# Four narrow constants put into one tile of a decoder layer kernel, which moves the wide tiles on the left side of SBUF by 64 bytes

## The chip, the cores and the metric

The kernel runs on one core of a Trainium2 chip. The metric is the device time of one execution in microseconds (us). Three runs of the kernel before gave 1234.45 us in the median (1233.17 to 1236.06); the execution that was profiled took 1231.72 us by the same clock and spans 1230.0 us in its trace.

## The reference

One layer of a decoder, for one sequence of 512 tokens of width 1024, all in float32:

```
h    = adaLN(rms_norm(x), c)
P    = h @ w_in                       # 1024 x 10016: attention, RWKV-7 and gate columns
y_a  = attention_mixer(P[att])  @ w_att_out   # three (window, dilation) groups, 8 heads of 64
y_r  = rwkv7_mixer(P[rwkv])     @ w_rwkv_out  # 16 heads of 64, delta-rule state
x    = x + gt1 * ((sig(g_a) * y_a + sig(g_r) * y_r) @ w_o)
h2   = adaLN(rms_norm(x), c)
u    = causal depthwise conv (width 3) of  h2 @ w_up      # 1024 x 5632
x    = x + gt2 * ((silu(u[gate]) * u[val]) @ w_down)      # 2816 x 1024
out  = rms_norm(x)
```

## The kernel before

**Products.** Every large product is split into high and low parts: an operand a is rounded to float32r as `ahi`, and `alo = a - ahi`; a product is three matmuls, hi by hi, hi by lo, lo by hi (`gemm_ks`, through the helper `mm` at L148, so all of them carry the line L148 and are told apart by their tiles). In a matmul one operand is stationary (128x128, loaded into TensorE beforehand by a weight load) and the other moves past it (up to 512 columns). The names in a row of the profile stand as out<-moving,stationary.

**Stages, in order of time.** Start (`start`): x is normed and transposed into `hhi`, `hlo`. Attention: products `qk` and `v` with w_in. RWKV: products `r`, `k`, `v`, gates (`pg`), then a chain of small matmuls per pair of heads. The output product of attention `pa` (moving `ahi`, `alo`) and of RWKV `pr` (moving `yhi`, `ylo`). The mix with w_o, called `o`. Then the up-projection `u`: `ffn_first` makes the first block of each half (moving `h2hi`, `h2lo`, stationary the weights), first for 384 of the 512 tokens, then for the last 128, and `ffn_up` the other 21 blocks of each half at 512 tokens: 21 x 2 x 8 x 3 = 1008 matmuls with 512 columns. Last the down-projection `o` (`ffn_down`): the weights move and `fhi`, `flo` are stationary. Weights come by DMA into `raw`, ScalarE rounds them into `whi`, VectorE subtracts into `wlo`.

**What sets the order.** Up to the mix a planner (`Plan`) with durations and priorities writes the order out; after it the order of the code holds. The change touches no task, duration or priority of it.

**Where tiles lie.** SBUF is given out by pools. Pools on the left side are stacked upwards, in the order in which they are opened, from the end of the constants (`cp`, the first pool). Pools on the right side are stacked downwards from byte 229,344 of a partition, which is 224 more than a multiple of 256. A tile takes its bytes per partition rounded up to 32, so a column of one float (4 bytes) takes 32. The wide tiles have sizes that are multiples of 256 bytes, so that all wide tiles behind one another share one offset modulo 256 bytes, which the narrow tiles ahead of them set.

On the left lie the weights of most products (`whi`, `wlo`, `raw` of the pool `wp`), `hhi`, `hlo`, `mhi`, `mlo`, `fhi`, `flo`. On the right lie `ahi`, `alo`, `yhi`, `ylo`, `h2hi`, `h2lo`, the rows of w_ada (`araw`), and the second weight buffer of `ffn_first` (pool `uw`, opened on the right): it holds the weights of the second half's first block, while those of the first half's first block are in `wp` on the left.

**The constants.** `ones` (one column of 1.0, stationary or moving in the small products with c), `mhalf` (-0.5, exponent of the inverse roots on GpSimd), `sel2` (two columns that pick a head) are tiles of `cp`; `half` is a tile of the pool `ip` on the left, made by one VectorE reduction (L1062).

**The last norm.** In `ffn_down` each block of 128 tokens has a narrow tile `ss` for sums of squares, in the pool `op` on the right, with 2 buffers.

Of the kernel before, what the change touches and what calls it, by code (L numbers as in the profile page):

```python
# [10 lines left out]
F32 = mybir.dt.float32  # L11
# [7 lines left out]
P = 128  # L19
# [109 lines left out]
class Layer:  # L129
# [72 lines left out]
    def consts(self):  # L202
        nc, ctx, tc = self.nc, self.ctx, self.tc
        self.cp = cp = ctx.enter_context(tc.tile_pool(name="cp", bufs=1))
        self.dr = ctx.enter_context(tc.tile_pool(name="dr", bufs=1, space=DRAM))
        self.ident = cp.tile([P, P], F32, name="ident")
        make_identity(nc, self.ident)
        self.ones = cp.tile([P, 1], F32, name="ones")
        nc.gpsimd.memset(self.ones, 1.0)
        self.mhalf = cp.tile([P, 1], F32, name="mhalf")  # L210
        nc.gpsimd.memset(self.mhalf, -0.5)

        self.cols = cp.tile([P, 4, P], F32, name="cols")
        self.col = {}


        self.mask = cp.tile([P, 2, P], F32, name="mask")
        self.cen = cp.tile([P, P], F32, name="cen")
        self.bones = cp.tile([P, P], F32R, name="bones")
        self.sel2 = cp.tile([P, 2], F32, name="sel2")  # L220

    def consts_rest(self):

# [817 lines left out]
    def rwkv(self, tail):  # L1041

        nc, tc, pl = self.nc, self.tc, self.pl
        self.cw, self.cps, self.ip, self.pps = [Late() for _ in range(4)]
        self.gps = [Late(), Late()]
        es, pre, even = self.rw_ctx, self.pre_ctx, ExitStack()

        def open_():
            self.att_ctx.close()
            pool = lambda st, room, name, bufs=1, **kw: setattr(  # L1050
                room, "pool", st.enter_context(tc.tile_pool(name=name, bufs=bufs, reuse_waits="tile", **kw)))
            pool(es, self.cw, "cw", 2)
            pool(es, self.gps[1], "gp1", 4)
            pool(es, self.cps, "cps", space=PSUM)
            pool(es, self.ip, "ip")
            pool(even, self.gps[0], "gp0", 4)
            pool(pre, self.pps, "pps", space=PSUM)

        def half():

            self.half = self.ip.tile([P, 2], F32, name="half")
            nc.vector.tensor_reduce(self.half, self.ident.rearrange("p (q s y) -> p s q y", q=4, s=2), axis=AX.XY,  # L1062
                                    op=ALU.add)
        self.opened = pl.add("NO", 0, open_, list(pl.tasks), name="open")
        self.y_d = self.dr.tile([P, KD, S], F32, name="y_d")
        self.halved = pl.add("DVE", 0.3, half, [self.opened], M_)
        self.prs = [[{}, {}] for _ in range(4)]
        self.grp = [{} for _ in range(4)]
        self.gd, self.gdt = {}, {}
        self.lora()  # L1070
        for g in range(4):
            for i in range(2):
                self.pair(g, i)
            self.inverse(g)
            self.chain(g)
        for m in range(2 * KD):
            self.early_gate(m)

        def close_pre():
            pre.close()  # L1080
            self.more = tail()

        def close_even():
            even.close()
            self.more()

        t0 = pl.add("NO", 0, close_pre, [t for t in pl.tasks if "pre" in t.marks])
        t1 = pl.add("NO", 0, close_even, [t0, self.grp[0]["all"][0], self.grp[2]["all"][0]])
        self.gates(t0)
        self.att_out(t1)  # L1090
        self.rwkv_ahead(t1)
        T = mybir.EngineType
        with tc.manual_schedule(engines={T.PE, T.DVE, T.Activation, T.Pool, T.SP}):
            pl.run()

    def psx(self, s):
        return self.pps.tile([P, 512], F32, tag="px", name=self.n(s), bufs=2)
# [944 lines left out]
    def ffn_down(self, xp, op, psx):  # L2042
        nc = self.nc
        g2 = xp.tile([P, D], F32, name="gt2b", tag="gb")
        nc.sync.dma_start(g2, self.ada2["gt2"].to_broadcast([P, D]))
        nf = op.tile([P, D], F32, name="nf", tag="nf", bufs=1)
        nc.sync.dma_start(nf, self.norm_f_w.unsqueeze(0).to_broadcast([P, D]))
        pt = [[psx("o") for _ in range(2)] for _ in range(NT)]
        fk = lambda k: (self.fhi[:, k, :], self.flo[:, k, :])
        last = NFF - 4  # L2050
        end = {}
        for k in range(last):
            w = {k: self.row_w(self.w_down[0], k)}
            if k >= last - 4:
                end[k + 4] = self.row_w(self.w_down[0], k + 4, pool=op, tag="we", bufs=4)
            for n in range(NT):
                self.tok_gemm(pt[n], n, fk, w, [k], NFF)
        w = end

        def finish(n, u, ss, cuts):  # L2060

            rs = op.tile([P, 1], F32, tag="rs", name=self.n("rs"))
            nc.gpsimd.tensor_tensor(rs, ss[1], ss[0], op=ALU.add)
            nc.gpsimd.tensor_tensor(rs, rs, self.mhalf, op=ALU.pow)
            for eng, c0, c1 in cuts:
                if eng == nc.vector:
                    nc.vector.tensor_scalar(u[:, c0:c1], u[:, c0:c1], rs, 0.0, op0=ALU.mult, op1=ALU.add)
                else:
                    nc.scalar.activation(u[:, c0:c1], u[:, c0:c1], AF.Copy, scale=rs)
                (nc.scalar if eng == nc.vector else nc.sync).dma_start(self.out[n * P : (n + 1) * P, c0:c1], u[:, c0:c1])  # L2070

        halves = [(nc.scalar, 0, 512), (nc.scalar, 512, 1024)]
        for n in range(NT):
            t = op.tile([P, D], F32, name=self.n("xo"), tag="xo")
            u = op.tile([P, D], F32, name=self.n("uo"), tag="uo", bufs=4)

            parts = [(0, 0, 512), (1, 512, 1024)] if n < NT - 1 else [(0, 0, 512), (1, 512, 768), (1, 768, 1024)]
            ss, sofar = op.tile([P, 3], F32, name=self.n("ss"), tag="ss2"), None
            acc = op.tile([P, 2], F32, name=self.n("ms"), tag="ms")
            for x, (hf, c0, c1) in enumerate(parts):  # L2080
                cs, ps, add = slice(c0, c1), pt[n][hf][:, c0 - 512 * hf : c1 - 512 * hf], self.x1[n][:, c0:c1]
                if x == 2:

                    nc.vector.tensor_tensor(add, t[:, cs], add, op=ALU.add)
                    ps = psx("o")[:, : c1 - c0]
                self.down(ps, n, fk, w, range(last, NFF), c0, c1, x == 2)
                if x == 1 and len(parts) == 3:
                    nc.vector.tensor_tensor(t[:, 512:], pt[n][hf], g2[:, 512:], op=ALU.mult)
                else:
                    nc.vector.tensor_tensor(t[:, cs], ps, g2[:, cs], op=ALU.mult)  # L2090
                nc.vector.tensor_tensor(t[:, cs], t[:, cs], add, op=ALU.add)
                jk = op.tile([P, 512], F32, name=self.n("jk"), tag="jk")
                nc.scalar.activation(jk[:, : c1 - c0], t[:, cs], AF.Square, scale=D ** -0.5, accum_out=ss[:, x : x + 1])
                nc.vector.tensor_tensor(u[:, cs], t[:, cs], nf[:, cs], op=ALU.mult)
                if x < len(parts) - 1:
                    nc.gpsimd.tensor_scalar(acc[:, x : x + 1], ss[:, x : x + 1], sofar if x else RMS_EPS, 0.0,
                                            op0=ALU.add, op1=ALU.add)
                    sofar = acc[:, x : x + 1]
                if x == 0 and n:
                    finish(*done)  # L2100
            done = (n, u, (sofar, ss[:, len(parts) - 1 : len(parts)]), halves)
        finish(*done[:3], [(nc.vector, 512, 1024), (nc.scalar, 0, 512)])
# [102 lines left out]
```

## Time and profile before

| | |
|---|---|
| median of three runs | 1234.45 us |
| the profiled execution: its own time / its span | 1231.72 us / 1230.0 us |
| TensorE (PE) busy | 1179.3 us, 96% of the span |
| VectorE (DVE) busy | 750.2 us, 61% |
| ScalarE (ACT) busy | 542.4 us, 44% |
| GpSimd (POOL) busy | 109.2 us, 9% |
| moved by DMA | 139.41 MB, 113 GB/s over the span |
| mean granted TensorE clock | 0.984 of full speed |

Matmuls overlap: a row of 394 ns says how long one is in the array, from its start to its modelled end, and the next one starts well before that. What a stream of matmuls costs is the spacing of their starts, which is read from the timeline, row against row, or from the length of a block in the chain of waits divided by its count.

### The profile page before, as it was taken

The numbers are of one execution on the slowest core, as the hardware profiler recorded it, in microseconds if no ns is written. First come the engines' busy times: TensorE is split into PE (matmuls) and PEld (weight loads), VectorE is DVE, ScalarE is ACT, GpSimd is POOL, SyncE is SP. The second block draws the span as 40 slices with busy tenths as digits, with TensorE's granted clock in tenths as the row PEclk, the third lists the DMA queues.
The fourth block names the chain that finished last, engine by engine and source line by source line (L and its number), as shares of the span: only waits on it lengthen the run. The fifth ranks groups of instructions, "written<-read, shape, count | busy, mean of one in ns | idle before, by whom it ended". The sixth has DMA issues, their size and how long they took to land.

```text
span 1230.0 us, 18481 instructions
## 1 busy us (share of the span) xinstructions
PE 1179.3 (96%) x7200; PEld 946.1 (77%) x7200; DVE 750.2 (61%) x1266; ACT 542.4 (44%) x1011; POOL 109.2 (9%) x228
## 2 busy tenths in 40 slices
PE   4999999999999999999999599999999999999997
PEld 3788887889778776767786467788888888878886
DVE  5687862431668977846896844764556556652135
ACT  4374521522565474465545443444444444442123
POOL 4000000000000013132103122014000000000001
PEclk9899999999999999999999799999999999999999
DMA  9845872120233342413241525460232323233331
GB/s 316 249 132 166 273 229 66 45 80 18 69 103 94 90 112 74 126 47 98 80 114 43 163 58 178 156 206 18 69 103 86 103 86 102 86 103 103 103 120 68
DMA packets 168902, 139.41 MB, mean 113 GB/s; under 512 B 8849, under 2 KB 150251, under 8 KB 168815
## 3 DMA queue, kind: packets, MB, share of 16 engines
q1 hardware_dynamic: 168671, 137.98, 37.0%
q8 instruction: 56, 0.92, 0.3%
q14 instruction: 31, 0.25, 0.1%
q10 hardware_dynamic: 144, 0.26, 0.1%
HBM read 127.65 MB, written 10.56 MB: 112 GB/s over the span
## 4 chain that ended last, share of the span: by engine, by line
PE 79%; DVE 11%; DMA 6%; ACT 2%; issue 2%; SPq 0%; POOL 0%; POOLq 0%; DVEq 0%; ACTq 0%
PE u L148 22%; PE o L148 13%; PE v L148 7%; PE pg L148 7%; PE qk L148 5%; DMA araw<-in_w_ada_dram 4%; PE k L148 3%; PE r L148 2%; PE pa L148 2%; PE pr L148 2%; PE early L148 2%; PE po L148 2%; PE xy L148 2%; PE pt L151 1%; DVE tt L1514 1%
## 5 line engine op out<-in xcount | busy, mean ns | idle before, releaser
L194 DVE TENSOR_TENSOR wlo<-raw,whi 128x1024 fp32r<-128x1024 f32 x65 | 79.7, 1225 | 146.7 <-ACT whi L193 146.6
L148 PE MATMUL u<-h2lo,whi 128*128 128x512 f32 (+2 forms) x368 | 142.3, 387 | 0.0
L148 PE MATMUL u<-h2hi,whi 128*128 128x512 f32 (+2 forms) x368 | 142.3, 387 | 0.0
L148 PE MATMUL u<-h2hi,wlo 128*128 128x512 f32 (+2 forms) x368 | 142.2, 386 | 0.0
L1136 ACT CAST whi<-raw 128x1024 fp32r<-128x1024 f32 (+2 forms) x73 | 72.5, 994 | 123.7 <-PE qk L148 49.5
L193 ACT CAST whi<-raw 128x1024 fp32r<-128x1024 f32 x65 | 68.2, 1049 | 106.5 <-PE o L148 53.7
L1139 DVE TENSOR_TENSOR wlo<-raw,whi 128x1024 fp32r<-128x1024 f32 (+2 forms) x73 | 83.7, 1149 | 19.1 <-ACT whi L1136 18.8
L148 PEld LDWEIGHTS u<-h2lo,whi 128*128 128x128 f32 x368 | 68.9, 187 | 16.0 <-POOL h2lo L405 0.2
L148 PEld LDWEIGHTS u<-h2hi,wlo 128*128 128x128 f32 x368 | 68.9, 187 | 15.5
L148 PEld LDWEIGHTS u<-h2hi,whi 128*128 128x128 f32 x368 | 68.9, 187 | 15.4
L2028 DVE SCALAR_TENSOR_TENSOR u<-u,cols,u 128x511 f32<-128x511 f32 x88 | 65.7, 747 | 4.3 <-ACT u L2026 2.7
L148 PE MATMUL qk<-hhi,wlo 128*128 128x512 f32 x160 | 64.0, 400 | 0.0
L148 PE MATMUL qk<-hlo,whi 128*128 128x512 f32 x160 | 63.6, 397 | 0.0
L148 PE MATMUL qk<-hhi,whi 128*128 128x512 f32 x160 | 63.5, 397 | 0.0
L148 PE MATMUL o<-whi,fhi 128*128 128x512 f32 x144 | 56.1, 390 | 0.3 <-DVE u L2028 0.3
L148 PE MATMUL o<-wlo,fhi 128*128 128x512 f32 x144 | 56.0, 389 | 0.0
L148 PE MATMUL o<-whi,flo 128*128 128x512 f32 x144 | 56.0, 389 | 0.0
L148 PE MATMUL pg<-hhi,wlo 128*128 128x512 f32 x128 | 51.8, 405 | 0.0
L148 PE MATMUL pg<-hlo,whi 128*128 128x512 f32 x128 | 51.7, 404 | 0.0
L148 PE MATMUL pg<-hhi,whi 128*128 128x512 f32 x128 | 51.7, 404 | 0.0
L810 DVE CUSTOM_DVE_ANT_0 sm<-sc,m 128x256 f32<-128x256 f32 (+1 forms) x64 | 23.9, 404 | 37.6 <-PE sc L148 36.5
L347 DVE SCALAR_TENSOR_TENSOR acc<-araw,cols,acc 128x1024 f32<-128x1024 f32 x28 | 35.8, 1280 | 17.2 <-DMA araw<-in_w_ada_dram 17.1
(414 smaller groups left out, 2778.3 us busy)
## 6 DMA issues: line engine op xcount, KB each, us to landing
raw<-in_w_in_dram SPq DMA_DIRECT2D x62, 512.0 KB
raw<-in_w_up_dram SPq DMA_DIRECT2D x44, 512.0 KB
araw<-in_w_ada_dram SPq DMA_DIRECT2D x32, 512.0 KB
raw<-in_w_down_dram SPq DMA_DIRECT2D x22, 512.0 KB
araw<-in_w_ada_dram SPq DMA_DIRECT2D x32, 256.0 KB
wvraw<-in_w_in_dram SPq DMA_DIRECT2D x20, 256.0 KB
gate_d<-gs SPq DMA_DIRECT2D x16, 256.0 KB
gate<-gate_d SPq DMA_DIRECT2D x16, 256.0 KB
```

The costliest lines, as they stand in the source:

```text
L148: return self.nc.tensor.matmul(out, lhsT, rhs, start=start, stop=stop)
L151: self.nc.tensor.matmul(out, in_, self.ident[: in_.shape[0], : in_.shape[0]], is_transpose=True, start=start, stop=stop,)
L193: self.nc.scalar.copy(hl[0], raw)
L194: (lo_eng or self.nc.vector).tensor_tensor(hl[1], raw, hl[0], op=ALU.subtract)
L347: nc.vector.scalar_tensor_tensor(d["acc"], raw, ck, d["acc"], op0=ALU.mult, op1=ALU.add)
L810: nc.vector.tensor_tensor_reduce(d["sm", h][:, :wd], d["sc"][h][:, :wd], m[:, 256 - wd : 256] if gi == 0 else m[:, :wd], 1.0, 3.0e38, op0= ...
L1136: nc.scalar.copy(d["w"][0], d["raw"])
L1139: nc.vector.tensor_tensor(d["w"][1], d["raw"], d["w"][0], op=ALU.subtract)
L1514: nc.vector.tensor_reduce(t[:, n0:, j - 1 : j + 1], x, axis=AX.X, op=ALU.add)
L2028: nc.vector.scalar_tensor_tensor(u[:, d:], pu[:, : S - d], ch(c), u[:, d:], op0=ALU.mult, op1=ALU.add)
```

## The change

The four narrow constants become columns of one tile `few` of 8 columns (32 bytes) in the pool `cp`; the three tiles of `cp` and the tile `half` of `ip` are gone. `ss` of the last norm gets 4 buffers of its tag in place of the pool's 2.

```diff
@@ consts
-        self.ones = cp.tile([P, 1], F32, name="ones")
+
+        few = cp.tile([P, 8], F32, name="few")
+        self.ones, self.mhalf, self.sel2, self.half = few[:, 0:1], few[:, 1:2], few[:, 2:4], few[:, 4:6]
         nc.gpsimd.memset(self.ones, 1.0)
-        self.mhalf = cp.tile([P, 1], F32, name="mhalf")
         nc.gpsimd.memset(self.mhalf, -0.5)
...
-        self.sel2 = cp.tile([P, 2], F32, name="sel2")
@@ rwkv, half
-            self.half = self.ip.tile([P, 2], F32, name="half")
             nc.vector.tensor_reduce(self.half, self.ident.rearrange("p (q s y) -> p s q y", q=4, s=2), axis=AX.XY,
                                     op=ALU.add)
@@ ffn_down
-            ss, sofar = op.tile([P, 3], F32, name=self.n("ss"), tag="ss2"), None
+            ss, sofar = op.tile([P, 3], F32, name=self.n("ss"), tag="ss2", bufs=4), None
```

What it does to places, by the allocation of the two built programs (first byte in a partition, and in brackets its remainder by 256):

| tiles | side | before | after |
|---|---|---|---|
| `whi`, `wlo`, `raw` of `wp` | left | 21,792 ... (32) | 21,728 ... (224) |
| `hhi`, `mhi`, `fhi` | left | 46,368 (32) | 46,304 (224) |
| `hlo`, `mlo`; `flo` | left | 62,752; 91,424 (32) | 62,688; 91,360 (224) |
| second and third weight buffers of `pr` in `ip` | left | 150,336 (64), 155,520 (128) | 150,240 (224), 155,424 (32) |
| `whi`, `wlo` of `uw` | right | 167,904, 172,000 (224) | the same |
| `ahi`, `alo`; `yhi`, `h2hi`; `ylo`, `h2lo` | right | 159,712, 167,904; 176,096; 192,480 (224) | the same |
| `araw` of the start | right | 202,720 ... (224) | the same |
| `wehi`, `welo`, `uo` of `op` | right | 147,232 ... (32) | 147,168 ... (224) |

The order of instructions on every engine stays as it was, but for two places. On VectorE, at the head of the RWKV stage, the reduction that makes `half` (the names are tiles; in brackets the engines that a row waits for). Before:

```order
L1149 SCALAR_TENSOR_TENSOR lt_3016<-lg_2908,mu_2_123,sh 32x512 [waits DVE_49]
L1173 TENSOR_SCALAR lt_3016<-lt_3016 32x512 [waits Activation_49]
L1163 TENSOR_TENSOR sg_94<-lt_3016,sg_94 32x512 [waits Activation_49]
L1062 TENSOR_REDUCE half<-ident 128x2 [waits PE_49]
L1139 TENSOR_TENSOR wlo_3053<-raw_2980,whi_3052 128x1024 [waits DMAHW6_49,PE_49,Activation_49]
```

After:

```order
L1148 SCALAR_TENSOR_TENSOR lt_3014<-lg_2906,mu_2_121,sh 32x512 [waits DVE_49]
L1172 TENSOR_SCALAR lt_3014<-lt_3014 32x512 [waits Activation_49]
L1162 TENSOR_TENSOR sg_92<-lt_3014,sg_92 32x512 [waits Activation_49]
L1061 TENSOR_REDUCE few<-ident 128x2
L1138 TENSOR_TENSOR wlo_3051<-raw_2978,whi_3050 128x1024 [waits DMAHW6_49,PE_49,Activation_49]
```

The reduction stands at the same place and has lost its wait for TensorE (the bytes of `half` had been used by an earlier tile). On SyncE's DMA queue, where the eight `gate` tiles come back from DRAM ahead of the RWKV output product (`early_gates`), a wait stands one load earlier. Before:

```order
L1832 DMA gate_7550<-gate_d_4805 128x512 [waits PE_49]
L1832 DMA gate_7551<-gate_d_4985 128x512
L1832 DMA gate_7552<-gate_d_6065 128x512 [waits Pool_49]
L1832 DMA gate_7553<-gate_d_6106 128x512
L1832 DMA gate_7554<-gate_d_6228 128x512 [waits DMAHW3_49]
```

After:

```order
L1831 DMA gate_7547<-gate_d_4802 128x512 [waits PE_49]
L1831 DMA gate_7548<-gate_d_4982 128x512 [waits Pool_49]
L1831 DMA gate_7549<-gate_d_6062 128x512
L1831 DMA gate_7550<-gate_d_6103 128x512
L1831 DMA gate_7551<-gate_d_6225 128x512 [waits DMAHW3_49]
```

The wait for GpSimd has moved from the third load to the second; the loads themselves are in the same order.

## The prediction, made before the result

> **What bounds the kernel now.** I read the page's busy times first, then the chain of waits in order of time, then the busy times by window, and last the timeline, row against row.
>
> ```profile
> PE 1179.3 (96%) x7200; PEld 946.1 (77%) x7200; DVE 750.2 (61%) x1266; ACT 542.4 (44%) x1011; POOL 109.2 (9%) x228
> PE 79%; DVE 11%; DMA 6%; ACT 2%; issue 2%; SPq 0%; POOL 0%; POOLq 0%; DVEq 0%; ACTq 0%
> ```
>
> TensorE is busy 96% of the span and holds 79% of the chain that ends last. So time is won or lost by how fast TensorE takes its stream, not by what the other engines do. The chain says in which blocks (start, length, what):
>
> ```profile
> 780.66 28.00 PE pr L148 x120
> ...
> 858.29 243.47 PE u L148 x1073
> ...
> 1105.68 113.84 PE o L148 x501
> ```
>
> The up-projection is one unbroken block of 243.47 us, the down-projection one of 113.84. The windows inside these two (length, busy time and count by engine, granted clock, DMA share, GB/s) tell whether anything else paces them; the first row is the start stage, used below:
>
> ```profile
> 5.00:20.00 15.00, 4.62 (x16) 3.26 (x16) 8.11 (x18) 8.35 (x12) 9.60 (x22) 1.00 1.06 361
> ...
> 866.00:1103.00 237.00, 237.00 (x1021) 190.08 (x1021) 140.48 (x171) 100.82 (x129) 0.00 (x0) 1.00 0.32 94
> 1106.00:1219.00 113.00, 113.00 (x500) 93.59 (x499) 37.83 (x40) 28.33 (x37) 2.19 (x7) 1.00 0.30 100
> ```
>
> In both TensorE is busy all the time at the full clock (1.00), with VectorE at 59% and 33%, DMA at 0.3. Yet the two do not run at one speed. Here are, of each, a matmul and the one 24 later (start, time in the array):
>
> ```profile
> 949.92 0.39 PE L148 MATMUL u<-h2hi,whi 128*128 128x512 f32 x1
> ...
> 955.52 0.39 PE L148 MATMUL u<-h2hi,whi 128*128 128x512 f32 x1
> ```
>
> ```profile
> 1149.99 0.39 PE L148 MATMUL o<-whi,fhi 128*128 128x512 f32 x1
> ...
> 1155.43 0.39 PE L148 MATMUL o<-whi,fhi 128*128 128x512 f32 x1
> ```
>
> In u: 5.60 us / 24 = 233.3 ns a matmul. In o: 5.44 / 24 = 226.7 ns. The same form, the same clock, 6.6 ns apart. The groups by form (count, busy us, mean ns in the array, which is the spacing plus some 161) give the same and add the products of the attention stage, where the activations move and the weights stand still, as in u:
>
> ```profile
> L148 PE MATMUL qk<-hhi,wlo 128*128 128x512 f32 x49 | 19.1, 389 | 0.0
> ...
> L148 PE MATMUL o<-wlo,fhi 128*128 128x512 f32 x140 | 54.5, 389 | 0.0
> ...
> L148 PE MATMUL u<-h2hi,whi 128*128 128x512 f32 x336 | 132.4, 394 | 0.0
> ```
>
> 389 for qk (taken from 240 to 275 us, where its stream is unbroken) and o, 394 for u. So it isn't which operand moves. What u has alone is a place: `h2hi` and `h2lo` lie on the right at remainder 224 by 256, its weights on the left at 32, a distance of 192. In qk and o both operands lie at 32, distance 0.
>
> **The same product at both distances.** `ffn_first` settles more than any comparison between stages. Its two halves move the same `h2hi`, `h2lo` with 384 columns; the first half's weights are in `wp` at 32 (distance 192), the second half's in `uw` at 224 (distance 0):
>
> ```profile
> 851.31 0.34 PE L148 MATMUL u<-h2hi,whi 128*128 128x384 f32 x1
> ...
> 854.32 0.34 PE L148 MATMUL u<-h2hi,wlo 128*128 128x384 f32 x1
> ```
>
> ```profile
> 858.48 0.34 PE L148 MATMUL u<-h2hi,wlo 128*128 128x384 f32 x1
> ...
> 861.08 0.34 PE L148 MATMUL u<-h2hi,wlo 128*128 128x384 f32 x1
> ```
>
> First half, 17 steps: 3.01 / 17 = 177.1 ns. Second half, 15 steps: 2.60 / 15 = 173.3 ns. So a moving operand at 224 is not slow in itself; it is slow against a stationary one at 32. Distances between have rows too. The third weight block of the RWKV product (stationary at 128 and 64, moving at 224, distances 96 and 160), and that product's later blocks (weights at 32, distance 192):
>
> ```profile
> 766.58 0.39 PE L148 MATMUL pr<-yhi,w 128*128 128x512 f32 x1
> ...
> 770.51 0.39 PE L148 MATMUL pr<-yhi,w 128*128 128x512 f32 x1
> ```
>
> ```profile
> 782.13 0.39 PE L148 MATMUL pr<-ylo,w 128*128 128x512 f32 x1
> ...
> 789.83 0.39 PE L148 MATMUL pr<-ylo,w 128*128 128x512 f32 x1
> ```
>
> 17 steps in 3.93 us are 231.2 ns; 33 steps in 7.70 us are 233.3 ns. By distance: 0 gives 226.7, 96 and 160 mixed 231.2, 192 gives 233.3 in two stages that share nothing but this.
>
> **The change part by part.**
>
> *Left tiles from 32 to 224.* Products with both operands on the left keep distance 0, and so 226.7. Products that move a right tile against a left one go from 192 to 0:
> - u, 1008 matmuls of 512 columns: 1008 x (233.3 - 226.7) = 6.65 us off the block of 243.47.
> - u, the first half's 24 of 384 columns: 24 x (177.1 - 173.3) = 0.09 us.
> - pr, the 120 in the block of 28.00 us: 120 x 6.6 = 0.79 us. The earlier pr matmuls stand between waits for weight loads, so they give nothing; and of the third block 16 go from distance 96 to 192, about 2 ns each: nothing.
> - pa, 96 matmuls between the small ones of the last RWKV chain. These are its rows:
>
> ```profile
> L148 PE MATMUL pa<-ahi,whi 128*128 128x512 f32 x32 | 14.3, 447 | 0.0
> ```
>
> At 447 in place of 389 it is held up by more than its distance: 0 to 96 x 6.6 = 0.63 us. I take the middle, 0.3.
>
> Sum: 6.65 + 0.09 + 0.79 + 0.3 = 7.8 us.
>
> **Does the gain reach the end?** In u nothing ends a wait of TensorE; what covers the rest is VectorE's 140 us and ScalarE's 101 in 237, and a DMA share of 0.32. 3% less time leaves VectorE at 61%. Behind u stand the split of the last weights and the last conv, then o at its old speed and an unchanged tail. So the 7.8 us go to the end whole.
>
> By the Trainium skill, "SBUF — State Buffer", section "Who interferes with whom", TensorE has two read ports, one for the moving operand and one for weight loads, independent of each other, and never waits on anyone. By that, distance would mean nothing and the sum would be 0. The 177.1 and 173.3 ns above disagree with it; I keep it as a rival.
>
> *DMAs into left tiles now land at 224.* The start stage has DMA at a share of 1.06 and 361 GB/s, mostly into `araw`, at 224 already: 340 GB/s for a full share. In the down-projection the weights land at 32: 100 / 0.30 = 333. So 224 is no slower, and I take 0. From below the bound is 0, from above the worst that the next part gives.
>
> *The constant tile.* Its memsets are the same in number and place, and the matmuls and inverse roots that read it wait as before. `half` loses a wait on VectorE, behind which the split of a weight block is queued:
>
> ```profile
> L1062 DVE TENSOR_REDUCE half<-ident x1: 289/289/289, 340.8 to 340.8; 128x2 f32<-128x128 f32 x1
> ```
>
> That view names no idle time of VectorE ahead of it and nobody who waited for it. Taken: 0; a gain is bounded by its own 0.29 us.
>
> *The `gate` loads.* The wait for GpSimd moves from the third of eight issues to the second. The row of the queue:
>
> ```profile
> 757.38 3.77 SPq L1832 DMA_DIRECT2D gate<-gate_d  x8
> ```
>
> Eight issues in 3.77 us, 0.47 us apart: no wait shows. One step earlier it may cost up to one step, 0.47 us, since the loads of w_rwkv_out queue behind it and TensorE waits for those; below nothing there is no reason. Taken: 0. *Four buffers of `ss`* remove a reuse that four blocks never stood in line for; taken 0, and what they do move is `wehi`, `welo` to 224 together with `fhi`, which keeps distance 0.
>
> **The time.** The profiled execution took 1231.72 us, 1.7 more than its span; less 7.8 gives 1223.9. It was faster than the median of the runs shown by 2.7 us, so for the median I forecast 1234.45 - 7.8 = 1226.7 us.
>
> **The rivals.**
>
> *The distance counts modulo 512 or more.* All rows of distance 0 above are also 0 modulo 512, while u goes from 192 to 256 modulo 512 (176,096 - 21,728 = 301 x 512 + 256), of which no stream is shown. For it: nothing excludes it. Against it: a small product of the RWKV stage moves `lw` at 32 against `l2h` at 192 on the right, at a distance of 352 modulo 512 and 96 modulo 256:
>
> ```profile
> L148 PE MATMUL pw<-lw,l2h x8: 394/394/499, 346.3 to 590.8; 128*128 128x512 f32 x8
> ```
>
> Its median of 394 ns is not what a place halfway back to a fast 512 would give; it goes with pr's third block at 96. Price: half the gap stays, 3.9 us off, 1230.6. Chance 0.10.
>
> *Distance means nothing* and something else sets u and pr apart from o and qk (their data, or PSUM read by VectorE): the change then doesn't do what it says, 1234.4 us. Against it stand the two halves of `ffn_first`, in the same 10 us. But those are 24 matmuls each. Chance 0.12.
>
> *A moving operand at 224 is slow, one at 32 fast.* Then u stays as it is and everything on the left falls to 233.3. On the page and in the groups alone these are qk 3 x 160, o 3 x 144 and pg 3 x 128 = 1296 matmuls:
>
> ```profile
> L148 PE MATMUL qk<-hhi,wlo 128*128 128x512 f32 x160 | 64.0, 400 | 0.0
> L148 PE MATMUL o<-whi,fhi 128*128 128x512 f32 x144 | 56.1, 390 | 0.3 <-DVE u L2028 0.3
> L148 PE MATMUL pg<-hhi,wlo 128*128 128x512 f32 x128 | 51.8, 405 | 0.0
> ```
>
> 1296 x 6.6 = 8.6 us more: 1243.0. It is slower from the first left product on, as none gains. For it: every slow stream moves a tile at 224. Against it: 173.3 ns at 224 on 224. Chance 0.06.
>
> *Loads at 224 are slower, in the start stage.* By the DMA issues
>
> ```profile
> raw<-in_w_in_dram SPq DMA_DIRECT2D x8, 256.0 KB
> wvraw<-in_w_in_dram SPq DMA_DIRECT2D x20, 256.0 KB
> ```
>
> the eight `raw` and, by the code, four of the `wvraw` belong to the start: 3 MB into left tiles, about 9 us at the 340 GB/s above. If each took a fifth longer, that is 1.8 us where DMA bounds, and the gain falls to 6.0: 1228.5. Chance 0.03. The Trainium skill, "DMA: Bandwidth & Descriptors", section "How a descriptor splits into AXI transactions", states the rule behind it: a descriptor that starts off a 256-byte boundary fetches from the boundary below and pays for the unused bytes, so that 224 wastes more than 32. The 340 against 333 GB/s does not bear it out.
>
> **How the numbers follow.** The forecast has 0.69. A measurement of this kernel can tell about 0.2%, 2.5 us, from no change. Faster: 0.69 + 0.10 + 0.03 = 0.82; within 0.2%: 0.12; slower: 0.06. The forecast's own range is 1224 to 1229.5: pa's and pr's bounds and the spread of the runs. The first and last rivals take the upper end to 1232; with the forecast these hold 8 in 10.
>
> **What would show it.** In the profile after: 24 matmuls of u in 5.44 us, 389 ns in its groups; the block of u 236.8 us, that of pr 27.2, that of o still 113.8; windows with TensorE busy throughout. If u reads 391 or 392, the distance counts modulo more than 256. If o and qk read 394, the place of the moving operand decides. If u stays at 394 and o at 389, the distance was never the cause. I would also be wrong if u got new idle time before its matmuls, or if the start stage grew.

## The result, and the profile after

| | before | after |
|---|---|---|
| median of 6 runs | 1232.39 us (1229.96 to 1236.06) | 1223.95 us (1219.20 to 1225.69) |
| the profiled execution: its own time / its span | 1231.72 / 1230.0 us | 1224.45 / 1222.7 us |
| ratio of the times, 95% interval | | 0.992 (0.9894 to 0.9947) |

The changed kernel is faster by 0.5 to 1.1%. The forecast was 1226.7 us in a range from 1224.0 to 1232.0: the measured median lies 0.05 us under the range. The blocks that carry the forecast came out as it said, and the number was set too high by what it was taken off from; both are shown below.

The page's busy times and the first row of its chain, after:

```profile
PE 1174.4 (96%) x7200; PEld 950.0 (78%) x7200; DVE 750.1 (61%) x1266; ACT 542.4 (44%) x1011; POOL 109.3 (9%) x228
PE 81%; DVE 10%; DMA 5%; ACT 2%; issue 1%; SPq 0%; POOL 0%; POOLq 0%; DVEq 0%; ACTq 0%
```

The same 7200 matmuls keep TensorE busy 4.9 us less, though u and pr below lost 7.5: elsewhere it was busy 2.6 us longer, part of which is shown further down. The other engines are where they were. The chain of waits after, in order of time (start, length, what), answers the three blocks of before:

```profile
776.29 4.48 PE o L148 x11
780.77 27.22 PE pr L148 x120
...
857.67 236.78 PE u L148 x1073
...
1098.38 113.86 PE o L148 x501
```

The block of u went from 243.47 to 236.78 us (forecast 236.8), that of pr from 28.00 to 27.22 (27.2), that of the down-projection stayed (113.84, now 113.86). The windows inside the last two (length, busy time and count by engine, granted clock, DMA share, GB/s) show no new wait and the same clock:

```profile
866.00:1095.00 229.00, 229.00 (x1012) 189.67 (x1012) 139.64 (x169) 100.09 (x128) 0.00 (x0) 1.00 0.33 97
1100.00:1212.00 112.00, 112.00 (x496) 92.73 (x495) 37.20 (x39) 27.78 (x36) 2.26 (x8) 1.00 0.30 99
```

In the timeline after, a matmul of u and the one 24 later stand 5.44 us apart, 226.7 ns each, where they were 5.60 us apart:

```profile
949.67 0.39 PE L148 MATMUL u<-h2hi,whi 128*128 128x512 f32 x1
...
955.11 0.39 PE L148 MATMUL u<-h2hi,whi 128*128 128x512 f32 x1
```

And the groups by form after, over the whole span (count, busy us, mean ns in the array):

```profile
L148 PE MATMUL u<-h2hi,whi 128*128 128x512 f32 x336 | 130.8, 389 | 0.0
...
L148 PE MATMUL qk<-hhi,wlo 128*128 128x512 f32 x160 | 64.3, 402 | 0.0
...
L148 PE MATMUL o<-whi,fhi 128*128 128x512 f32 x144 | 56.1, 390 | 0.3 <-DVE u L2027 0.3
```

u fell from 394 to 389 ns, while o (390) stayed and qk reads 402 after 400 (pauses included), though both their operands moved from 32 to 224. The 2 ns of qk don't come from the place: with the buffers of `ss` undone, further down, both operands are still at 224 and qk reads 400. That ends two rivals: a moving operand at 224 is not slow, and 256 bytes modulo 512 is not a slow distance.

**What came earlier ahead of pr was lost again.** The two profiled executions differ by 7.27 us, u and pr together by 7.47. The rest are small differences of both signs, outside the blocks. The chain before, with the last load that pr's weights wait for and the first matmuls of the mix:

```profile
763.18 7.63 DMA raw<-in_w_rwkv_out_dram
...
777.65 3.00 PE o L148 x11
```

and after:

```profile
760.78 8.68 DMA raw<-in_w_rwkv_out_dram
```

The load came 2.40 us earlier and ended 1.35 us earlier, and the eleven matmuls began 1.36 us earlier (777.65 to 776.29); then they took 4.48 us in place of 3.00, so that pr began 0.11 us later than before. The window over those (columns as above), first before, then after:

```profile
777.00:780.00 3.00, 2.66 (x11) 1.64 (x10) 2.78 (x4) 1.32 (x2) 0.00 (x0) 1.00 0.38 130
```

```profile
777.00:780.00 3.00, 3.00 (x9) 1.93 (x8) 2.28 (x3) 1.22 (x2) 0.00 (x0) 0.56 0.53 175
```

The granted clock was 0.56 there, against 1.00. So u began 0.62 us earlier (858.29 to 857.67), most of pr's 0.78, and the end moved by 7.3: of that the block of u is 6.69. The experiments tell whether the change has to do with that clock.

### The profile page after: what moved, and what is told of

Same layout as the page of the kernel before. It is cut to its first block, busy times and chain, and to the rows that moved or that the text cites. A ratio compares the mean times of both kernels' runs of the same rounds, so it can differ in the third digit from the quotient of the medians.

```text
span 1222.7 us, 18481 instructions
## 1 busy us (share of the span) xinstructions
PE 1174.4 (96%) x7200; PEld 950.0 (78%) x7200; DVE 750.1 (61%) x1266; ACT 542.4 (44%) x1011; POOL 109.3 (9%) x228
## 4 chain that ended last, share of the span: by engine, by line
PE 81%; DVE 10%; DMA 5%; ACT 2%; issue 1%; SPq 0%; POOL 0%; POOLq 0%; DVEq 0%; ACTq 0%
PE u L148 22%; PE o L148 13%; PE v L148 8%; PE pg L148 7%; PE qk L148 7%; PE r L148 3%; PE k L148 3%; PE pa L148 2%; PE pr L148 2%; DMA araw<-in_w_ada_dram 2%; PE po L148 2%; PE xy L148 2%; PE pt L151 2%; PE early L148 1%; PE sc L148 1%
```

## The experiments

The first three were timed together on one chip, beside 17 runs of the kernel before: 1231.59 us in the median (1228.38 to 1235.48). Where a short diff says "before", it is made on the kernel before.

### The changed kernel again

> The changed kernel once more, on one chip with the next two and with the kernel before. Distance theory (the spacing of the starts of matmuls depends on how far apart moving and stationary operand start, modulo 256 bytes): block of u 236.8 us, of pr 27.2 us, and 7.5 us less than the kernel before, give or take 2. Rival (part of the 8.4 us came from the spread of the start stage and of the granted clock): the blocks read the same, but the whole difference comes out nearer to 7 than to 9, and single executions of either kernel spread by 5 us or more.

Median of 6 runs: 1224.99 us (1220.97 to 1226.93), ratio 0.9942 (0.9922 to 0.9962). Its chain:

```profile
776.75 4.38 PE o L148 x11
781.13 27.21 PE pr L148 x120
...
858.04 236.78 PE u L148 x1073
...
1098.75 113.83 PE o L148 x501
```

The blocks repeat within 0.03 us, while the totals of the six runs spread over 6 us. What differs from run to run lies outside them.

### The left side moved back, all else kept

```diff
@@ after, consts
         few = cp.tile([P, 8], F32, name="few")
         self.ones, self.mhalf, self.sel2, self.half = few[:, 0:1], few[:, 1:2], few[:, 2:4], few[:, 4:6]
+        cp.tile([P, 16], F32, name="pad")
```

An unused tile of 64 bytes puts the left tiles back at 32; the one tile of constants and the four buffers of `ss` stay.

> The changed kernel with an unused tile of 64 bytes behind the constant tile: the constants stay in one tile and the four buffers of ss stay, but the wide left tiles are back at 32. Distance theory: u at 233.3 ns a matmul, its block 243.5 us, pr 28.0, the time within 1.5 us of the kernel before. Rival (the constants in one tile or the buffers of ss gained something): the time stays below that of before by more than 2 us although u reads 233.3.

Median of 12 runs: 1231.64 us, ratio to before 1.0007 (0.9994 to 1.002). The whole gain is gone, and u and pr stand at before's numbers:

```profile
776.93 2.89 PE o L148 x11
779.82 28.00 PE pr L148 x120
...
857.47 243.47 PE u L148 x1073
...
1104.86 114.38 PE o L148 x501
```

The constants in one tile, the lost wait, the moved wait of the `gate` loads and the buffers of `ss` are together worth nothing that these runs can tell. The down-projection even grew by 0.54 us: `wehi`, `welo` stay at 224 while `fhi` is back at 32, for 84 matmuls, 6.4 ns each.

### The other side moved

```diff
@@ before
     x1p = ctx.enter_context(pool("x1p", side="right"))
+    under = ExitStack()
+    under.enter_context(pool("under", side="right")).tile([P, 48], F32, name="pad")
     hp2 = pool("hp2", side="right")
...
     hp2.__exit__(None, None, None)
+    under.close()
```

192 unused bytes under `h2hi`, `h2lo` put these two at 32, where the left weights of before are. Nothing else of before is changed; `yhi`, `ylo` are freed by then and stay at 224.

> The kernel before, nothing of the change in it, with an unused tile of 192 bytes on the right under h2hi and h2lo: these go from 224 to 32, where the left weights are, and yhi, ylo, ahi, alo stay at 224. Distance theory: u at 226.7 ns, its block 236.8 us, pr as before at 28.0 us; 6.7 us less than before. Rival (224 is a good place for the left tiles, or for all): u stays at 233.3 and the time at that of before.

Median of 6 runs: 1224.36 us, ratio 0.9941 (0.992 to 0.9962).

```profile
777.45 4.46 PE o L148 x11
781.92 27.99 PE pr L148 x120
...
859.60 236.81 PE u L148 x1073
...
1100.34 113.83 PE o L148 x501
```

u is as fast as in the changed kernel, with both operands at 32 in place of 224; pr, whose operands did not move, stays slow. So no place is good or bad: the distance between the two is. Here too the eleven matmuls took 4.46 us.

### A map of distances

A kernel of its own, with nothing but streams of 18 float32r matmuls behind a warm-up of 60:

```python
for i in range(8):
    for j in range(8):
        ps = stream(f"m{LET[i]}s{LET[j]}", 8 * i, 8 * j)   # first column of moving, of stationary
for j in range(32):
    ps = stream(f"f{LET[j]}", 0, 4 * j)
```

> Matmuls alone: 18 of 128x512 float32r per stream, moving and stationary operand each at 0, 32, ... 224 bytes past a common multiple of 256 (64 streams, named m and s with a letter each, a for 0 to h for 224), then the stationary operand alone at 0, 16, ... 496 (32 streams, f). Nothing else runs. The kernel computes nothing of the reference. Distance theory: the diagonal of the 64 reads 389 ns in the array and 226.7 ns of spacing, whichever the place; off the diagonal the reading depends on the difference alone, 394 at 192; and among the 32, the streams 256 bytes apart read the same. Rival (the slower spacing needs the other engines at work, as it had in u and pr): all streams read the same. Rival (the distance counts modulo 512): the streams at 256 to 496 read otherwise than those at 0 to 240.

The groups by form (the names: m, the moving operand's place, s, the stationary one's, a to h for 0, 32 ... 224 bytes; f and a letter: the moving operand at 0, the stationary one at 0, 16, 32 ... for a, b, c ...):

```profile
L34 PE MATMUL fg<-mv,st 128*128 128x512 f32 x18 | 4.4, 396 | 0.0
...
L34 PE MATMUL fe<-mv,st 128*128 128x512 f32 x18 | 4.4, 395 | 0.0
...
L34 PE MATMUL fc<-mv,st 128*128 128x512 f32 x18 | 4.4, 395 | 0.0
...
L34 PE MATMUL fm<-mv,st 128*128 128x512 f32 x18 | 4.3, 392 | 0.0
...
L34 PE MATMUL mcsc<-mv,st 128*128 128x512 f32 x18 | 4.2, 389 | 0.0
L34 PE MATMUL fb<-mv,st 128*128 128x512 f32 x18 | 4.2, 389 | 0.0
...
L34 PE MATMUL fq<-mv,st 128*128 128x512 f32 x18 | 4.2, 389 | 0.0
```

389 at distance 0 (mcsc: both at 64), 16 (fb) and 256 (fq); 395 at 32 (fc) and 64 (fe), 396 at 96 (fg), 392 at 192 (fm). The spacing of the starts, averaged over the last nine steps of each stream, by the distance from the moving to the stationary operand in bytes:

| distance | 0 | 16 | 32 | 64 | 96 | 128 | 160 | 176 | 192 | 208 | 224 | 240 | 256 | 272 | 288 |
|---|---|---|---|---|---|---|---|---|---|---|---|---|---|---|---|
| ns | 226.7 | 226.7 | 233.6 | 233.1 | 234.3 | 233.8 | 233.3 | 229.9 | 228.9 | 233.3 | 233.1 | 226.7 | 226.7 | 226.7 | 233.4 |

From 256 to 496 the row of 0 to 240 is repeated. In the 8 x 8 grid of both places the diagonal has 226.7 everywhere, and the other entries go by the difference alone, to about 2 ns. The period is 256 bytes, the fast places reach 16 to either side, and 192 is better than the rest. No other engine worked meanwhile, and nothing but the places of TensorE's own two operands differs between the streams: the slower pace needs nothing else. Before, u was at 32 - 224 + 256 = 64 in this table, after at 0. (The prediction counted the other way round, from the stationary to the moving operand: its 192 is the table's 64, its 96 and 160 are 160 and 96.)

### The map's 192 and 96, put into the kernel

```diff
@@ before, as above
+    under.enter_context(pool("under", side="right")).tile([P, 32], F32, name="pad")
```

> The kernel before with an unused tile of 128 bytes under the right pools: h2hi, h2lo, yhi, ylo lie at 96 by 256, the left weights stay at 32, so the moving operand lies 64 bytes behind the stationary one. The matmul map alone gave 229.1 ns at this distance (192 from stationary to moving), where 0 gave 226.6 and most others 233.4. If the map carries over to the kernel, the block of u is between the two: 243.47 - 1008 x (233.3 - 229.1) = 239.2 us, a matmul of u 229.1 ns apart. If in the kernel only distance 0 is fast and all else alike slow, 243.5 us. If only the offset of one side counts, 243.5 too, or 236.8. One look; the total should be some 4 us under the kernel before.

The pad lies under h2 alone, so that `yhi`, `ylo` stay at 224, other than the text says, and pr has to stay. Measured, in one run: 1226.32 us, against 1234.95 for one run of the kernel before. These 8.6 us are more than the block explains (4.5): two single runs can't tell, the block can.

```profile
779.71 27.99 PE pr L148 x120
...
857.34 239.00 PE u L148 x1073
```

239.00 against the map's 239.2. With a pad of 32 bytes ([P, 8]) the distance is 96, the map's worst:

> The kernel before with an unused tile of 32 bytes under the right pools: h2hi, h2lo, yhi, ylo lie at 192 by 256, the left weights at 32, the stationary operand 96 bytes past a moving one (distance 160 from left to right). The map gave its highest spacing here, 234.3 ns against 233.4. If the map carries over, the block of u is 243.47 + 1008 x 0.9 ns = 244.4 us, longer than in the kernel before; if all distances other than 0 are alike, 243.5. One look; a total cannot tell 1 us, the block can.

```profile
780.38 27.99 PE pr L148 x120
...
858.02 244.42 PE u L148 x1073
```

244.42 against 244.4, longer than before: distances other than 0 are not alike, and a table made with matmuls alone gives a block of 240 us in the full kernel to 0.2 us. The total, 1232.39 us, can't tell 1 us.

### The buffers of ss, undone

```diff
@@ after, ffn_down
-            ss, sofar = op.tile([P, 3], F32, name=self.n("ss"), tag="ss2", bufs=4), None
+            ss, sofar = op.tile([P, 3], F32, name=self.n("ss"), tag="ss2"), None
```

> The changed kernel with two buffers of ss in the last norm again, as before: one part of the change undone. wehi and welo, the stationary or moving tiles of the last four blocks, then lie at 160 by 256 while fhi lies at 224. By the distance theory u stays at 236.8 us and pr at 27.2, and the block of o grows from 113.86 by 84 x 2.3 ns (if the map's 64-byte dip applies) to 84 x 6.7 ns: 114.05 to 114.4 us. If the buffers of ss gave part of the gain by taking away a wait, the tail behind the last matmul grows by the wait instead, some tenths of a us, and o stays.

One run took 1224.58 us. Its chain, with the last product of the tail:

```profile
857.67 236.78 PE u L148 x1073
...
1098.38 114.02 PE o L148 x501
...
1218.54 0.72 ACT uo L2068
```

The pool lies on the right and grows downwards, so with 64 bytes less `wehi`, `welo` lie at 32, as before the change, and not at 160, as the text says; against `fhi` at 224 that is the map's 192. o grew from 113.86 to 114.02 us, 0.16 as 84 matmuls there give it (84 x 2.2 ns = 0.18). From its end to the last `uo` are 6.14 us, and 6.15 in the changed kernel, where `uo` starts at 1218.39. So the four buffers take away no wait; they add 64 bytes, and these keep `wehi`, `welo` in step with `fhi`.

### Own weights or the next ones; widths and types

Matmuls alone again; a pair is the first column of the moving and of the stationary operand, of 4 bytes each:

```python
pairs("own", [(0, 0), (16, 16)], 36)
pairs("next", [(0, 16), (16, 0)], 36)
pairs("both", [(0, 16), (0, 16)], 36)
```

> Matmuls alone; nothing of the reference is computed. Three streams of 36 tell which reading meets the moving one. Stream own: each matmul's moving operand at distance 0 to its own weights, 64 bytes off from the next one's; next: 64 bytes off from its own weights, at 0 to the next one's; both: always 64 off. If the weight load that runs while a matmul streams (the next one's) is what collides, own is slow (233) and next fast (226.6). If it is a matmul's own pair, the reverse. both is slow either way (233.4). Streams ea to ef (4, 8, 12, 20, 24, 28 bytes off): with a window of 16 bytes up to and with 16, ea to ec are 226.6 and ed to ef slower, with a smooth edge they lie between. With 384, 256 and 128 columns: if the load of 128 columns collides only while it runs, the loss a matmul stays near 6.7 ns whatever the width, as the 3.8 ns at 384 columns in the kernel do not quite say; if it goes with the columns that stream, it falls to 5, 3.3 and 1.7 ns. bfloat16 (ha to hh) and plain float32 (ga to gh 128 columns, ka and kc 512): no theory; alike at every distance if it is a matter of float32r's reads alone.

```profile
L46 PE MATMUL ka<-xin 128*128 128x512 f32 x36 | 15.6, 592 | 0.0
L46 PE MATMUL kc<-xin 128*128 128x512 f32 x36 | 15.6, 592 | 0.0
...
L46 PE MATMUL next<-mv,st 128*128 128x512 f32 x36 | 8.6, 396 | 0.0
L46 PE MATMUL both<-mv,st 128*128 128x512 f32 x36 | 8.6, 394 | 0.0
L46 PE MATMUL own<-mv,st 128*128 128x512 f32 x36 | 8.5, 394 | 0.0
...
L46 PE MATMUL hb<-bm,bs 128*128 128x512 bf16 x18 | 4.0, 379 | 0.0
```

Neither reading was right: own (spacing 231.7 ns) and next (233.3) are both slow, as both is (233.3). The next experiment gives a reason for own. For next it gives none: there each weight load starts 2 to 4 ns behind the start of the matmul ahead of it, and lies at distance 0 to what that one streams. In these two streams the places also change from each matmul to the next, so which pair meets stays open. Plain float32 (429.2 ns at 0 and at 64 bytes; 111.7 at all eight distances with 128 columns) and bfloat16 (215.8 at all eight) know no distance. With float32r the gap is 6.6 ns at 512 columns, 3.2 at 384 (173.4 and 176.6, and 3.8 in the kernel); at 256 (119.4 and 117.8) and 128 (111.7 and 111.6) it is no loss at all. Steps that are not multiples of 16 bytes are slow inside the window too: 232.4, 230.4 and 230.0 ns at 4, 8 and 12 bytes.

### Short runs of wide matmuls

```python
for j, k in enumerate((3, 5, 10, 20)):
    runs(f"r{LET[j]}z", k, 0, 8, 3)      # 8 times: k wide at distance 0, then 3 narrow
    runs(f"r{LET[j]}y", k, 8, 8, 3)      # the same at 8 columns, 32 bytes
pairs("keep", [(0, 0)], 48)
ps = pairs("turn", [(0, 0)] * 12 + [(0, 8)] * 12, 96)
```

> Matmuls alone; nothing of the reference is computed. It asks why pa gave nothing. Runs of 3, 5, 10 and 20 wide float32r matmuls, each followed by 3 narrow plain float32 ones, at distance 0 (raz, rbz, rcz, rdz) and at 32 bytes (ray, rby, rcy, rdy). Theory: the fast pace is a state that a stream falls into, which in the map took up to seven matmuls after a switch of places. Then runs of 3 and 5 at distance 0 are no faster than at 32 (within 1 ns a matmul; or up to some 2), runs of 20 keep over half of the 6.7 ns. Rival: each matmul is fast by its own and the next one's place alone; then a run of 5 keeps four fifths or more, 5 ns a matmul, and pa's gain was lost elsewhere. Stream keep: 48 at 226.6 ns. Stream turn, 12 at 0, 12 at 32 bytes in turn: by the theory the last matmul at distance 0, beside which the first weights at 32 are loaded, is already slow (235), the 12 at 32 are at 233.4, and the first up to seven at 0 vary and average some 231, then 226.6; by the rival all 11 at 0 are at 226.6.

The groups (ray, raz: runs of 3; rby, rbz: 5; rcy, rcz: 10; rdy, rdz: 20; y at 32 bytes, z at 0; three runs of raz, nine matmuls, came straight behind the warm-up with nothing narrow between, which lowers the mean of raz):

```profile
L50 PE MATMUL rdy<-mv,st 128*128 128x512 f32 x160 | 39.2, 399 | 0.0
L50 PE MATMUL rdz<-mv,st 128*128 128x512 f32 x160 | 38.6, 395 | 0.0
...
L50 PE MATMUL rcy<-mv,st 128*128 128x512 f32 x80 | 20.6, 403 | 0.0
L50 PE MATMUL rcz<-mv,st 128*128 128x512 f32 x80 | 20.5, 402 | 0.0
...
L50 PE MATMUL rby<-mv,st 128*128 128x512 f32 x40 | 11.2, 410 | 0.0
L50 PE MATMUL rbz<-mv,st 128*128 128x512 f32 x40 | 11.2, 410 | 0.0
...
L50 PE MATMUL ray<-mv,st 128*128 128x512 f32 x24 | 7.6, 426 | 0.0
...
L50 PE MATMUL raz<-mv,st 128*128 128x512 f32 x24 | 6.9, 409 | 0.0
```

Runs of three win some 10 ns in all, where 3 x 6.7 would be 20: from the first start to the last end 940 ns in the median of the last five, and 950 at 32 bytes. That is more than was expected of them. Runs of five are no faster at distance 0: 1404 ns, and 1404 at 32 bytes. Runs of ten win 7 ns in all (2563 and 2570), runs of twenty 74 (4830 and 4904), where 20 x 6.7 would be 134. The steps inside a run at distance 0 show why: 314, 235, 233, 236, 224, 231, 236, 228, 233, 231, and only from there on 226 and 227. Behind narrow matmuls the fast pace is a state that a stream falls into after some ten. In the stream that turns every 12 matmuls from 0 to 32 bytes, the last one at 0, beside which the first weights at 32 are loaded, already takes 235, as expected; but back at 0 it took one slow step (231), not up to seven, so how long the way back is depends on the phase in which the stream was.

## Why the prediction was right, and where it was wrong

*The bound* and *the cause* were right. TensorE's pace set the time, and the distance between the two operands, modulo 256, set the pace of u. Shown from both sides (the left moved, the right moved, the left moved back) and by two other distances of u in the kernel (192 and 96 in the map).

*The terms.* u's 6.65 us measured 6.69 (the first half's 24 matmuls stand outside that block). pr's 0.79 measured 0.78. pa's 0.3 measured nothing, though its row needs care:

```profile
L148 PE MATMUL pa<-ahi,whi 128*128 128x512 f32 x32 | 14.5, 453 | 0.0
```

453 ns after, 447 before, but 445 in the second profile of the changed kernel and 454 with the right side moved, where pa's places are those of before. What moves the row is the clock. In all eight profiles of the full kernel the granted clock is 0.50 over a stretch that ends at 711 to 713 us, just after pa has begun; 9 of the 96 matmuls started in it after, 6 in the second profile and 7 before. The others stood in the array for 421.8, 420.7 and 422.0 ns in the mean, a gain of 0.1 us at most. The step said that pa is held up by more than its distance and took the middle between 0 and 0.63; the lower end was right. TensorE gets pa in runs of at most six, once eight, between other matmuls, and the runs of three, five and ten above won 10, 0 and 7 ns each, where 6.7 ns a matmul would be 20, 34 and 67. The terms taken at 0 (the tile of constants, the `gate` loads, `ss`) held: the kernel with the left side moved back has all of them and is at 1.0007 of before. Loads at 224 are answered among the rivals. The prediction's row for 96 and 160 mixed, 231.2, is not in the map, which has 233.3 and 234.3 for the two; there two places alternated, as in own (231.7). No term rested on it. The sum, made right, is 6.65 + 0.09 + 0.79 = 7.5 in place of 7.8.

*The step that failed is the base*: "It was faster than the median of the runs shown by 2.7 us, so for the median I forecast 1234.45 - 7.8 = 1226.7 us." That took the median of three runs for the kernel's level and the profiled 1231.72 for a fast exception. It was the other way round: six runs gave 1232.39 in the median, seventeen others 1231.59. Of the 2.7 us between forecast and measurement the base makes 2.06 (1234.45 - 1232.39); the other 0.6 is that the two medians differ by 8.44, more than the 7.8 of the sum and the 7.5 of the blocks. That is spread: beside the seventeen runs the same kernel gave 6.6. From the profiled execution's own time the sum gives 1223.9 us; that this comes within 0.05 of the measured 1223.95 is luck, since the sum was 0.3 too high for pa and the medians of six runs move by more. The range had the same fault: its low end of 1224.0 lay even above the profiled time less the sum, though single runs of one kernel spread over 7 us (1228.38 to 1235.48), and the median of the three used lay 2.9 above that of the seventeen.

*The rivals.* That distance means nothing falls: 226.7 and 233.6 ns with nothing else at work. By the Trainium skill, "SBUF — State Buffer", section "Who interferes with whom", TensorE's two read ports are independent and it never waits; for wide float32r matmuls these runs do not bear that out. Modulo 512 falls in the changed kernel and in the map, the place of the moving operand with o and qk. Slower loads at 224 would hold up all that lies ahead of the mix, and nothing was: by the timelines its first matmul came between 774.9 and 775.2 us in the three kernels with the left side at 224, and between 774.6 and 776.1 in the five with it at 32.

*The end of the chain* moved by as much as the blocks, as said, but for the half clock over the first `o`. It is in the profiles of the changed kernel (4.48 and 4.38 us for eleven matmuls), of it without the buffers of `ss`, and of before with 192 or 32 bytes under h2 (4.46 and 4.25 us); it is missing before, with 128 bytes (2.93 us) and with the left side moved back (2.89). With pr fast or slow it comes or not; so the place of the tiles alone doesn't make it; whether the change favours it (three of three profiles with the left side at 224, two of five with it at 32) is open. The traces show what goes with it. The granted clock changes in steps of 3.41 us, on a grid that lies differently in each execution, and the half clock lasts one step here. TensorE waits ahead of the first `o` for the rounded weights of w_o (1.03 us before, 2.34 after, 1.38 in the second profile of the changed kernel). In the five profiles with the half clock it was busy for 1.20 to 1.70 us of the step of 3.41 ahead of it; in the three without, for 1.86 to 2.05 us of the step that holds the same wait. So the length of that wait, and whether it falls into one step or is cut by the grid, seem to decide; no run tests it.

## What to carry to other kernels

Where a long stream of float32r matmuls with 512 columns loads weights for each, look at the bytes at which its two operands start: a difference of 0 or 16 bytes to either side of a multiple of 256 gave 226.7 ns, most others 233 to 234, 3% more, in streams of twenty and more, and a pad of some bytes is all that it costs. Compare the spacing of the starts of one form between stages; a few ns that no wait explains is a place, and a pad on either side tests it. For a base, take the profiled execution and the median of all the runs there are, and keep their spread in the range.

## What the runs showed of the hardware

- Wide float32r matmuls run at 226.7 ns at best here, bfloat16 ones, also with a weight load each, at 215.8, plain float32 at 429.2; only the first knows the distance, among those tried.
- The distance acts with a period of 256 bytes; 16 bytes to either side are free (4, 8 and 12 are not), 192 costs 2.2 ns a matmul, 176 costs 3.2, all other steps of 16 bytes 5 to 8.
- The fast pace takes up to ten matmuls to settle behind narrow ones and is lost with the first weights that are loaded at another distance. What inside TensorE or SBUF does this, no run shows.
- The granted clock falls to 0.50 in stretches that are multiples of 3.41 us (one at about 777 us in five of eight profiles, seven or eight up to 711 to 713 us in all). At 777 us it went with a step before it in which TensorE was busy for at most 1.70 of 3.41 us. Such a stretch moves the mean of a row by more than the distance does in short runs (pa, 453 and 445 ns in one kernel).
